# Seven-product units in the first halves alone, and their weight sums as VectorE additions

## The chip, the core and the metric

The kernel runs on one core of a Trainium2 chip, in one launch. A core has TensorE (the matrix multiplier, PE in the profile; PEld is its loading of stationary operands), VectorE (DVE), ScalarE (ACT), GpSimd (POOL) and SyncE (SP), which here only issues transfers. Each engine works through its own instructions in order and waits for others by semaphores. Transfers from the device's main memory are issued from the queues of SP and POOL (a few from ACT) and carried by 16 DMA engines. Matrix products accumulate in PSUM; everything else lies in SBUF. The metric is the device time of an execution in microseconds (us).

## The reference

A bidirectional encoder of two layers on a sequence of 256 tokens of width 2048, in 32-bit floats. Layer 0 mixes tokens by grouped-query attention with rotary positions, layer 1 by dilated windowed attention. Both are followed by the same kind of gated MLP, which is where the change lies:

```
def conv_ffn(h, w_up, conv_w, conv_b, w_down):
    u = h @ w_up                       # [256, 2048] @ [2048, 2 * 5632]
    u = lax.conv_general_dilated(u, conv_w[:, None, :], window_strides=(1,), padding=((1, 1),),
                                 dimension_numbers=('NWC', 'WIO', 'NWC'), feature_group_count=c) + conv_b
    gate, val = jnp.split(u, 2, axis=-1)
    return (jax.nn.silu(gate) * val) @ w_down      # [256, 5632] @ [5632, 2048]

h = h + conv_ffn(rms_norm(h, ffn_norm[i]), w_up[i], conv_w[i], conv_b[i], w_down[i])
```

After the second layer a last RMS norm gives the output.

## The kernel before

**Splitting.** A 32-bit product is made of three products of rounded operands. Each weight tile `raw` (128 partitions x 1024 numbers, 512 KB) is split by ScalarE into a rounded high part `wh` and by VectorE into the rest, `wl = raw - wh`. Each operand of the activations is split once in the same way (`xh`, `xl`). TensorE then adds `xh*wh`, `xh*wl` and `xl*wh`, three matmuls of 128 x 128 by 128 x 512 each. `wh` and `wl` have four buffers each (`NHL`). In the down-projections the raw tiles have six buffers: four, and two more that every third tile takes (`raw_tile`), so a load may be issued once the tile six places ahead of it is used up.

**An ordinary chunk.** `feed` (L102) multiplies a group of 512 rows of a weight matrix ("chunk", `kg`) with one group of 512 columns (`n`). It loads two raw tiles (L114), splits them (L136, L137) and issues 24 matmuls, 12 for each raw tile ("half chunk"; L124 to L126).

**The MLP.** `ffn` (L371) runs the 11 blocks of the inner width in two halves of 6 and 5 (`HALVES`, loop variable `hf`). In each half the blocks are projected up, convolved and gated; the value blocks' results become the stationary operands (`act_split`, L463), and the down-projection of this half follows, four groups of 512 columns that are added to the residual `h`. The work of the activations is written as generators. A matmul stream calls `step` between chunks, which issues the next piece of such work, so that it runs beside the matmuls.

**The seven-product unit.** For a chunk in `fast` (chunks 2 and 3), the pair of column groups `ns` is not done by two times 24 = 48 matmuls. The activations' chunk and the two weight chunks are taken as 2 x 2 blocks, and the eight block products are replaced by seven, of combined operands, in the manner of Strassen and Winograd: 42 matmuls. The activations' combinations are made once (`combined`, L481). The weights' blocks are b11, b12, b21, b22, and four sums of them are needed: t1 = b11 + b12, t3 = b12 + b22, t2 = t1 + b22, t4 = t2 + b21. `fast_unit` (L506) makes the unit in the order b11, b21, b22, t1, t3, t2, t4: a split by ScalarE (L534) and VectorE (L535) and six matmuls (L540 to L542) for each. The seven accumulators are folded into `h` later (`fold`, L546).

t1 and t3 are made by transfers: `load_sum` (L512) loads one block from SP's queue (L509) and then lets a transfer from POOL's queue add the other block on top of it (L514). t2 and t4 are VectorE additions (L531, L533). t1, t2 and t4 lie in the tiles `u` that are free at that time.

**Order.** `pair` (L570) sets the order of chunks for a pair of column groups. In the first half (`hf == 0`) of both layers, for each of two pairs: chunks 0 and 1 ordinary on both sides (eight half chunks), unit of chunk 2, chunk 4 ordinary on both sides (four half chunks), unit of chunk 3, chunk 5 ordinary. That makes eight units. In the second half of layer 1 alone (`last`), the first pair of column groups has two units more, with ordinary chunks between them; `plain_too` (L498) then makes plain halves of these chunks' activations too, for the column groups 2 and 3, which run ordinarily (`project` and, for the last, `project_last`). The second half of layer 0 has no units: `project2` runs column groups 0 and 1, `project` 2 and 3.

The order of instructions on each engine is not that of the text. A scheduler places them when the program is built, by priorities (`tc.high_priority(offset=AHEAD)` lifts the splits and the sums beside them) and by a model of when operands and buffers come free. `tc.keep_in_program_order` ties the places of single instructions.

Of the kernel before, what the change touches and what calls it, by code (L numbers as in the profile page):

```python
# [30 lines left out]
def tile_encoder(ctx: ExitStack, tc: tile.TileContext, x, xT, w_a, w_ao, q_gain, k_gain, w_b, w_bo,  # L31
                 rel_bias, gains, w_up, conv, w_down, final_norm, rope, ident_c, onehot, out):
    nc = tc.nc
# [211 lines left out]
    def pair_slot(kt, shape, dt=F32, name="pr"):  # L245
        return hpool.tile(shape, dt, tag=f"a{kt // 2}", name=nm(name))
# [124 lines left out]
    def ffn(l, hT, ss_in, cw, g_next, last, side=None):  # L371
        with tc.tile_pool(name=nm("fpool"), bufs=1) as fp:
# [90 lines left out]
            def act_split(value):  # L463
                slots, k0 = value[5:]
                cv = value[2]
                if k0 // 4 in fast:
                    slots[-1 - k0 // 4], *rest = combined(cv, k0)
                    if hf == 1:
                        plain_too(k0, 20 + 2 * fast.index(k0 // 4), *rest)
                    ready.add(k0 // 4)  # L470
                    yield
                    return
                for j in range(4):
                    hi, lo = slots[k0 + j]
                    tc.keep_in_program_order(nc.scalar.activation(hi, cv[:, j, :], AF.Copy))
                    nc.vector.tensor_tensor(lo, cv[:, j, :], hi.bitcast(F32), ALU.subtract)
                    if j == 1:
                        yield
                ready.add(k0 // 4)

            def combined(cv, k0):  # L481
# [14 lines left out]
                return pick, v, sx  # L496

            def plain_too(k0, spot, v, sx):  # L498
                c = pair_slot(spot, [P, 2, 2, P], F32R, "c")
                split_in_order(c[:, 0], c[:, 1], v[:, 0, :, 1])  # L500
                for kt in range(4):
                    b, j = divmod(kt, 2)
                    one = (sx[:, 4, j], sx[:, 5, j]) if b else (c[:, 0, j], c[:, 1, j])
                    slots[k0 + kt] = (sx[:, b, j], one[0]), (sx[:, 2 + b, j], one[1])

            def fast_unit(acc, pick, wap0, wap1, begun, end):  # L506
                def load(wap, i, r=None):
                    r = r or raw_tile()
                    nc.sync.dma_start(r.rearrange("p a c -> p (a c)"), wap[:, i * 1024:(i + 1) * 1024])  # L509
                    return r  # L510

                def load_sum(wapx, i, wapy, k, r=None):  # L512
                    r = load(wapx, i, r)
                    nc.gpsimd.dma_start(r.rearrange("p a c -> p (a c)"), wapy[:, k * 1024:(k + 1) * 1024],  # L514
                                        accum_op=ALU.add)
                    return r

                def spot(i):
                    return u_tile(i)[:, :1024].rearrange("p (a c) -> p a c", a=2)

                t1 = load_sum(wap0, 0, wap1, 0, spot(0))
                b11 = load(wap0, 0)
                t3 = load_sum(wap1, 0, wap1, 1)
                b21, b22 = load(wap0, 1), load(wap1, 1)
                t2, t4 = spot(1), spot(2)
                for i, (q, r) in enumerate(((1, b11), (2, b21), (3, b22), (5, t1), (7, t3), (6, t2), (4, t4))):
                    wh = spool.tile([P, 2, 512], F32R, tag="wh", name=nm("wh"), bufs=NHL)
                    wl = spool.tile([P, 2, 512], F32R, tag="wl", name=nm("wl"), bufs=NHL)
                    with tc.high_priority(offset=AHEAD):
                        if q == 6:  # L530
                            nc.vector.tensor_tensor(t2, t1, b22, ALU.add)  # L531
                        if q == 4:
                            nc.vector.tensor_tensor(t4, t2, b21, ALU.add)  # L533
                        nc.scalar.activation(wh, r, AF.Copy)  # L534
                        nc.vector.tensor_tensor(wl, r, wh.bitcast(F32), ALU.subtract)  # L535
                    xh, xl = pick[q]
# [33 lines left out]
            def pair(wd, ns, lhs, order, done, hurry=False):  # L570
# [4 lines left out]
                for i, (kg, side) in enumerate(order):  # L575
# [22 lines left out]
                        if pending:  # L598
                            step()
                    if end:  # L600
                        while beside and hf == 1:
                            step(True)
                        done(sides[side], ns[side])

            def flush(value):
# [12 lines left out]
            for hf, (p0, p1) in enumerate(HALVES):  # L618
                slots = {}
                ready.clear()  # L620
                new_us()
                fast = (2, 3) if hf == 0 or last else ()
                last_value = None
                for p in range(p0, p1):
                    k0 = 4 * (p - p0)
# [107 lines left out]
                if hf == 0:  # L733
                    for ns in (0, 1), (2, 3):
                        pair(wd, ns, slots, both[0] + both[1] + f0 + both[4] + f1 + both[5], done, ns[0] == 0)
                    continue
# [609 lines left out]
```

## Time and profile before

| | us |
|---|---|
| median of three runs | 2271.96 |
| lowest, highest | 2268.68, 2272.84 |
| profiled execution | 2274.03 |
| its span, first to last instruction | 2272.2 |
| TensorE with a matmul in work | 2241.3 (99%) |
| VectorE busy | 1688.0 (74%) |
| ScalarE busy | 1266.0 (56%) |
| GpSimd busy | 756.2 (33%) |

All figures of views come from the one profiled execution. Its mean granted TensorE clock is 0.995. Matmuls overlap: a row gives about 390 ns for one, but they start some 227 ns apart, so rates are to be taken from starts and not from durations. A busy TensorE is therefore one that has no hole, not one at its peak. "Busy" of an engine leaves out what its queue does, such as issuing transfers. A time in brackets behind a row of the timeline is idle time of that engine just before it, and what ended it.

### The profile page before, as it was taken

How to read it: one execution, taken by the hardware profiler on the slowest of the kernel's cores; microseconds unless marked ns; L12 is line 12 of the kernel's file. 1: busy time of each engine (PE TensorE's matmuls, PEld its weight loads, DVE VectorE, ACT ScalarE, POOL GpSimd, SP SyncE). 2: the span in 40 equal slices, each digit the busy share in tenths (PEclk: the TensorE clock that was granted, in tenths of full speed). 3: DMA queues.
4: the chain of work that ended last, by engine and by line, in shares of the span. 5: the costliest groups of instructions: out<-in, count | busy, mean ns of one | idle time of the engine just before them, and what ended most of it. 6: DMA issues, size and time to landing. Idle time of an engine off the chain costs nothing.

```text
span 2272.2 us, 28705 instructions
## 1 busy us (share of the span) xinstructions
PE 2241.3 (99%) x10029; PEld 1852.9 (82%) x10029; DVE 1688.0 (74%) x2251; ACT 1266.0 (56%) x1754; POOL 756.2 (33%) x991
## 2 busy tenths in 40 slices
PE   9999999999999999999999999999999989999998
PEld 7888888887778888888888888888888877888877
DVE  6877867776766776878887887676768777676784
ACT  7576556556545656555454554445656645465653
POOL 3342065671006553010061007003666400356611
PEclk9999999999999999999999999999999999999999
DMA  8665665657766665566656555566655677565674
GB/s 302 193 216 179 216 196 189 194 194 210 241 220 191 194 194 194 186 196 200 185 189 194 186 176 177 184 203 201 200 196 193 204 232 231 192 196 192 215 230 135
DMA packets 130369, 455.30 MB, mean 200 GB/s; under 512 B 14760, under 2 KB 18600, under 8 KB 130224
## 3 DMA queue, kind: packets, MB, share of 16 engines
q1 hardware_dynamic: 124496, 434.30, 58.2%
q0 software_dynamic: 5440, 18.88, 4.2%
q8 instruction: 78, 1.28, 0.2%
q14 instruction: 67, 0.55, 0.1%
q10 hardware_dynamic: 288, 0.30, 0.0%
HBM read 448.07 MB, written 5.34 MB: 200 GB/s over the span
## 4 chain that ended last, share of the span: by engine, by line
PE 89%; DMA 4%; DVE 3%; POOL 2%; issue 1%; ACT 1%; SPq 0%; DVEq 0%; POOLq 0%; ACTq 0%
PE acc L125 28%; PE acc L124 28%; PE acc L126 28%; DMA u<-in_w_down_dram 2%; POOL wide L272 2%; DMA raw<-in_w_down_dram 1%; DVE wl L535 1%; DVE wl L137 1%; DMA raw<-in_w_a_dram 1%; PE ps L541 1%; PE ps L542 0%; PE acc L541 0%; PE ps L540 0%; ACT wh L136 0%; PE acc L542 0%
## 5 line engine op out<-in xcount | busy, mean ns | idle before, releaser
L137 DVE TENSOR_TENSOR wl<-raw,wh 128x1024 fp32r<-128x1024 f32 (+1 forms) x764 | 952.3, 1252 | 396.0 <-ACT wh L136 391.2
L136 ACT ACTIVATE wh<-raw 128x1024 fp32r<-128x1024 f32 (+1 forms) x764 | 799.5, 1050 | 707.0 <-PE acc L126 629.0
L124 PE MATMUL acc<-wh,xh 128*128 128x512 f32 x2176 | 849.6, 391 | 0.0
L125 PE MATMUL acc<-wl,xh 128*128 128x512 f32 x2176 | 848.8, 390 | 0.7 <-DVE wl L137 0.6
L126 PE MATMUL acc<-wh,xh 128*128 128x512 f32 x2176 | 848.6, 390 | 0.0
L432 POOL COPY u<-quad 32x256 f32<-32x256 f32 x672 | 477.3, 710 | 340.2 <-DVE quad L268 313.8
L125 PEld LDWEIGHTS acc<-wl,xh 128*128 128x128 f32 x2176 | 409.2, 188 | 85.4 <-DVE wl L137 2.4
L126 PEld LDWEIGHTS acc<-wh,xh 128*128 128x128 f32 x2176 | 409.0, 188 | 84.9
L124 PEld LDWEIGHTS acc<-wh,xh 128*128 128x128 f32 x2176 | 409.5, 188 | 83.7 <-ACT wh L136 0.3
L124 PE MATMUL acc<-wh,a 128*128 128x512 f32 x824 | 321.5, 390 | 0.5 <-ACT wh L136 0.5
L125 PE MATMUL acc<-wl,a 128*128 128x512 f32 x824 | 321.0, 390 | 0.0
L126 PE MATMUL acc<-wh,a 128*128 128x512 f32 x824 | 321.0, 390 | 0.0
L124 PEld LDWEIGHTS acc<-wh,a 128*128 128x128 f32 x824 | 154.7, 188 | 32.4 <-ACT wh L136 0.8
L126 PEld LDWEIGHTS acc<-wh,a 128*128 128x128 f32 x824 | 154.7, 188 | 32.2 <-DVE a L219 0.2
L125 PEld LDWEIGHTS acc<-wl,a 128*128 128x128 f32 x824 | 154.8, 188 | 31.8 <-DVE wl L137 0.2
L272 POOL COPY wide<-quad 32x256 f32<-32x256 f32 x165 | 107.2, 650 | 171.8 <-DVE quad L268 162.7
L368 ACT ACTIVATE stg<-acc,rstd 128x512 f32<-128x512 f32 x122 | 82.8, 684 | 32.8 <-PE acc L126 32.8
L449 POOL TENSOR_TENSOR cv<-cg,cv 128x1024 f32<-128x1024 f32 x18 | 57.9, 3216 | 108.3 <-DVE cv L419 108.3
L419 DVE SCALAR_TENSOR_TENSOR cg<-u,cw,cg 128x256 f32<-128x256 f32 x176 | 82.2, 511 | 4.5 <-ACT cg L411 4.5
L402 POOL MEMSET u<- 128x4 f32 x12 | 1.0, 106 | 228.9 <-ACT junk L258 188.3
L419 DVE SCALAR_TENSOR_TENSOR cv<-u,cw,cv 128x256 f32<-128x256 f32 x176 | 73.7, 478 | 2.8 <-ACT cv L411 2.7
L534 ACT ACTIVATE wh<-raw 128x1024 fp32r<-128x1024 f32 x40 | 42.2, 1058 | 51.7 <-PE acc L126 23.5
(246 smaller groups left out, 1684.4 us busy)
## 6 DMA issues: line engine op xcount, KB each, us to landing
raw<-in_w_up_dram SPq DMA_DIRECT2D x352, 512.0 KB, 4.6
raw<-in_w_down_dram SPq DMA_DIRECT2D x176, 512.0 KB, 4.8
raw<-in_w_b_dram SPq DMA_DIRECT2D x144, 512.0 KB, 4.3
raw<-in_w_bo_dram SPq DMA_DIRECT2D x48, 512.0 KB, 3.8
raw<-in_w_a_dram SPq DMA_DIRECT2D x40, 512.0 KB, 4.7
raw<-in_w_ao_dram SPq DMA_DIRECT2D x32, 512.0 KB, 4.4
raw<-in_w_down_dram POOLq DMA_DIRECT2D x10, 512.0 KB, 8.8
u<-in_w_down_dram SPq DMA_DIRECT2D x10, 512.0 KB, 5.9
```

The source lines that it names most:

```text
L124: nc.tensor.matmul(accs[m], xh, wh[:, j, :], start=st, stop=False)
L125: nc.tensor.matmul(accs[m], xh, wl[:, j, :], start=False, stop=False)
L126: nc.tensor.matmul(accs[m], xl, wh[:, j, :], start=False, stop=sp)
L136: nc.scalar.activation(wh[:, c], r[:, c], AF.Copy)
L137: nc.vector.tensor_tensor(wl[:, c], r[:, c], wh[:, c].bitcast(F32), ALU.subtract)
L272: nc.gpsimd.tensor_copy(o[32 * c:32 * c + 32, :, 32 * q:32 * q + 32], quad[32 * q:32 * q + 32, c])
L368: nc.scalar.activation(o[:, m, :], accs[m], AF.Copy, scale=rstd[:, m:m + 1])
L419: nc.vector.scalar_tensor_tensor(cj, halves(flat[:, j, o:o + NT])[:, ::-1], tap(n, j, i), cj, ALU.mult, ALU.add)
L432: nc.gpsimd.tensor_copy(o, src)
L449: made.append(eng.tensor_tensor(cv, cg, cv, ALU.mult).ins)
L534: nc.scalar.activation(wh, r, AF.Copy)
L535: nc.vector.tensor_tensor(wl, r, wh.bitcast(F32), ALU.subtract)
```

## The change

Three things are changed.
- Layer 1's second half has no units any more. `fast` is empty there, and its down-projection takes the way of layer 0's second half: `project2` for column groups 0 and 1, `project` for 2; `project_last` stays for 3. `plain_too` goes.
- In the eight units left, no transfer adds. A unit loads its four blocks once each from SP's queue, in the order b11, b21, b22, b12.
- All four sums are VectorE additions, written directly in front of the split that reads them: t1 into a `u` tile, b12 + b22 in place of b12, t2 and t4 into `u` tiles. The order of the seven products is the same.

```
     if k0 // 4 in fast:
-        slots[-1 - k0 // 4], *rest = combined(cv, k0)
-        if hf == 1:
-            plain_too(k0, 20 + 2 * fast.index(k0 // 4), *rest)
+        slots[-1 - k0 // 4] = combined(cv, k0)
...
 def fast_unit(acc, pick, wap0, wap1, begun, end):
...
-    def load_sum(wapx, i, wapy, k, r=None):
-        r = load(wapx, i, r)
-        nc.gpsimd.dma_start(r.rearrange("p a c -> p (a c)"), wapy[:, k * 1024:(k + 1) * 1024],
-                            accum_op=ALU.add)
-        return r
...
-    t1 = load_sum(wap0, 0, wap1, 0, spot(0))
-    b11 = load(wap0, 0)
-    t3 = load_sum(wap1, 0, wap1, 1)
-    b21, b22 = load(wap0, 1), load(wap1, 1)
-    t2, t4 = spot(1), spot(2)
-    for i, (q, r) in enumerate(((1, b11), (2, b21), (3, b22), (5, t1), (7, t3), (6, t2), (4, t4))):
+    b11, b21, b22, b12 = load(wap0, 0), load(wap0, 1), load(wap1, 1), load(wap1, 0)
+    t1, t2, t4 = (spot(i) for i in range(3))
+    sums = {5: (t1, b11, b12), 7: (b12, b12, b22), 6: (t2, t1, b22), 4: (t4, t2, b21)}
+    for i, (q, r) in enumerate(((1, b11), (2, b21), (3, b22), (5, t1), (7, b12), (6, t2), (4, t4))):
...
         with tc.high_priority(offset=AHEAD):
-            if q == 6:
-                nc.vector.tensor_tensor(t2, t1, b22, ALU.add)
-            if q == 4:
-                nc.vector.tensor_tensor(t4, t2, b21, ALU.add)
+            if q in sums:
+                nc.vector.tensor_tensor(*sums[q], ALU.add)
             nc.scalar.activation(wh, r, AF.Copy)
             nc.vector.tensor_tensor(wl, r, wh.bitcast(F32), ALU.subtract)
...
-    fast = (2, 3) if hf == 0 or last else ()
+    fast = (2, 3) if hf == 0 else ()
...
     if not fast:
         done(project2(wd, 0, 1, slots, rest, 1, lambda a: done(a, 0)), 1)
         for n in (2, 3):
-            done(project(wd, n, slots, rest), n)
+            if last and n == 3:
+                project_last(wd, n, slots, rest, first_out, last_out)
+            else:
+                done(project(wd, n, slots, rest), n)
         continue
...
-    pair(wd, (0, 1), slots, both[0] + [(1, 0)] + f0 + [(1, 1)] + f1 + both[4], done, True)
-    done(project(wd, 2, slots, list(range(np_))), 2)
-    project_last(wd, 3, slots, list(range(np_)), first_out, last_out)
```

More of the change, by code (lines that the diff above doesn't have):

```diff
@@ L495, in combined, with load @@
                     pick[q] = own[0][:, i], own[1][:, i]
[L496 to L504, printed above, removed]
+                return pick
             def fast_unit(acc, pick, wap0, wap1, begun, end):
-                def load(wap, i, r=None):
-                    r = r or raw_tile()
+                def load(wap, i):
+                    r = raw_tile()
                     nc.sync.dma_start(r.rearrange("p a c -> p (a c)"), wap[:, i * 1024:(i + 1) * 1024])
-                    return r
-                def load_sum(wapx, i, wapy, k, r=None):
-                    r = load(wapx, i, r)
-                    nc.gpsimd.dma_start(r.rearrange("p a c -> p (a c)"), wapy[:, k * 1024:(k + 1) * 1024],
-                                        accum_op=ALU.add)
                     return r
@@ L600, in pair @@
                     if end:
-                        while beside and hf == 1:
-                            step(True)
                         done(sides[side], ns[side])
```

6 lines of the change are left out of this document (2 added, 4 removed).

## The prediction

> **What bounds the kernel now.** I read the page first, then the busy sums of the ten stretches in which the seven-product units run, then the timeline of one of them, the waits, and the landings of the loads.
>
> The page, span and engines:
>
> ```profile
> span 2272.2 us, 28705 instructions
> ...
> PE 2241.3 (99%) x10029; PEld 1852.9 (82%) x10029; DVE 1688.0 (74%) x2251; ACT 1266.0 (56%) x1754; POOL 756.2 (33%) x991
> ```
>
> TensorE is the bound: only 31 us of the span are without a matmul. So the change is worth what it does to the number of matmuls and to the holes between them. The holes sit in the units. Busy sums by stretch; each of the first ten runs from a unit's first matmul to the one behind its last, the eleventh is ordinary work:
>
> ```profile
> core 0: us, PE busy (x) PEld busy (x) DVE busy (x) ACT busy (x) POOL busy (x), PEclk, DMA share, GB/s
> 542.69:557.48 14.79, 11.62 (x43) 8.87 (x42) 9.18 (x9) 7.00 (x7) 0.89 (x1) 0.88 0.60 165
> 568.39:580.12 11.73, 10.18 (x44) 7.74 (x42) 11.73 (x12) 7.93 (x8) 0.00 (x0) 1.00 0.79 258
> 612.83:622.50 9.67, 9.67 (x44) 7.90 (x42) 9.10 (x9) 7.45 (x7) 0.86 (x1) 1.00 0.91 286
> 633.41:647.00 13.59, 10.19 (x44) 7.74 (x42) 12.82 (x12) 8.84 (x9) 0.32 (x3) 1.00 0.52 186
> 1816.91:1833.32 16.41, 12.54 (x43) 9.40 (x42) 9.54 (x10) 7.08 (x7) 1.72 (x2) 0.79 0.61 167
> 1844.23:1857.86 13.63, 11.62 (x43) 8.66 (x42) 13.17 (x12) 8.86 (x9) 0.35 (x1) 0.87 0.68 225
> 1890.53:1900.20 9.67, 9.67 (x44) 7.90 (x43) 7.46 (x7) 7.43 (x7) 1.72 (x2) 1.00 0.80 252
> 1911.10:1922.55 11.45, 10.20 (x44) 7.74 (x42) 11.45 (x11) 7.92 (x8) 0.32 (x3) 1.00 0.59 191
> 2167.38:2180.63 13.25, 11.28 (x46) 8.04 (x44) 12.35 (x15) 7.97 (x11) 0.92 (x2) 1.00 0.64 211
> 2185.64:2198.63 12.99, 10.83 (x43) 7.51 (x42) 10.14 (x10) 7.38 (x8) 0.00 (x0) 1.00 0.82 260
> 800.00:1000.00 200.00, 200.00 (x884) 165.66 (x883) 151.63 (x214) 115.44 (x162) 57.45 (x76) 1.00 0.59 191
> ```
>
> Two units run without a hole: 42 matmuls in 9.67 us. The eight of the first halves (layer 0, then layer 1) take 100.94 us together, 23.6 more than eight times 9.67. Ordinary matmuls follow each other every 200 / 883 = 0.2265 us, also in the second half of layer 0, which the last row crosses and which has no units. What makes the holes is seen in the first unit (timelines of SP, POOL, VectorE, TensorE):
>
> ```profile
> 536.91 0.33 SPq L509 DMA_DIRECT2D u<-in_w_down_dram  x1
> 542.74 0.89 POOL L514 DMA_DIRECT2D u<-in_w_down_dram  x1 [12.43 <-DVE wl L535]
> 548.26 1.23 DVE L531 TENSOR_TENSOR u<-u,raw 128x1024 f32<-128x1024 f32 x1 [5.54 <-DMA u<-in_w_down_dram]
> 549.46 0.51 PE L540 MATMUL ps<-wh,s 128*128 128x512 f32 x1 [2.42 <-ACT wh L534]
> 550.72 0.79 PE L541 MATMUL ps<-wl,s 128*128 128x512 f32 x1 [0.76 <-DVE wl L535]
> ```
>
> The sum t1 is a load from SP and behind it an adding transfer from POOL. Issued at 542.74, it lands 5.5 us later; VectorE, in order, stands before t2 (L531) for it, ScalarE before the split, TensorE behind both. By the waits this is the rule in the units:
>
> ```profile
> DVE u L531 <- DMA u<-in_w_down_dram: 31.4, 6, 8.3
> DVE u L531 <- DMA raw<-in_w_down_dram: 25.4, 4, 8.2
> ```
>
> All ten L531 waited for a transfer, 5.7 us each on average.
>
> **The change part by part.**
>
> *Second half of layer 1 without units.* Two units, 84 matmuls, become 96 ordinary ones: 96 x 0.2265 = 21.7 us. Their stretches last 13.25 + 12.99 = 26.24, less two ordinary matmuls inside the first (44 weight loads, not 42), 0.45: 25.8. Gain 4.1 us, in which 12 more matmuls (2.7) are already paid. The outer work that goes (combining the activations, a copy of their plain halves, folding the accumulators) and what replaces it (eight plain splits) lie beside some 10.9 us of matmuls per chunk (48 x 0.2265) and count nothing; if that cover were short it would be a row or two of VectorE, about 1 us. The order that takes their place is that of layer 0's second half, which had no hole in the row above; bound 0 to 2 us.
>
> *Transfers.* In the eight units left, each issues four loads from SP where it had five and none from POOL where it had two adding ones. Nothing on POOL's queue or on SP's waits behind them any more. A b11 tile now comes free after t1 instead of after its split, and so the second next chunk's load starts later; that load is needed a whole unit later and hides.
>
> *VectorE.* Per unit 7 splits + 4 sums instead of 7 + 2. Rows: three splits in a row, then the first unit as it ran (VectorE, and one ScalarE):
>
> ```profile
> 611.21 3.49 DVE L535 TENSOR_TENSOR wl<-raw,wh 128x1024 fp32r<-128x1024 f32 x3
> 536.75 1.22 DVE L535 TENSOR_TENSOR wl<-raw,wh 128x1024 fp32r<-128x1024 f32 x1
> 537.89 1.22 DVE L449 TENSOR_TENSOR cv<-cg,cv 128x1024 f32<-128x1024 f32 x1
> 539.03 1.22 DVE L535 TENSOR_TENSOR wl<-raw,wh 128x1024 fp32r<-128x1024 f32 x1
> 540.16 1.43 DVE L476 TENSOR_TENSOR a<-cv,a 128x256 fp32r<-128x256 f32 x4
> 541.50 1.22 DVE L535 TENSOR_TENSOR wl<-raw,wh 128x1024 fp32r<-128x1024 f32 x1
> 540.39 1.05 ACT L534 ACTIVATE wh<-raw 128x1024 fp32r<-128x1024 f32 x1
> ```
>
> One whole-tile operation every 1.14 us: 11 x 1.14 = 12.5 us for a unit of 9.67. VectorE loses 2.9 us per unit and must bring it as a lead. It has one: four split buffers let it stand three splits ahead, and a sum needs no split buffer, so it fills the time VectorE waits for one (an ordinary half chunk is 12 x 0.2265 = 2.72 us of TensorE for 1.14 of VectorE). In the built order the sums do not stand directly in front of their splits in every unit:
> - First unit of each layer: split 1, the product cv (L449), t1, split 2, an a split, t3, split 3, three a splits, split of t1, t2, split of t3, t4, split 6, split 7. From the row at 536.75 split 6 ends after 11 large ones and four a's: 536.75 + 11 x 1.14 + 1.43 = 550.7; TensorE, which began the unit at 542.69, takes 9.67 / 7 = 1.38 us per product and wants the low half of the sixth one matmul behind its start: 542.69 + 5 x 1.38 + 0.23 = 549.8. Hole about 1.0 us where there were 5.12 and 6.74; split 7, at 551.9, is in time again.
> - Second unit of the first pair: t1 comes behind split 1, then six more operations up to the split of t1, which is wanted 4.4 us into the unit. 7 x 1.14 + 0.08 = 8.1, so the last load must have landed 3.7 us before the unit begins. It takes the buffer of the second half chunk behind the first unit, split two operations after split 7 (551.9 + 2 x 1.14 = 554.2), and the unit begins at 542.69 + 9.67 + 1.0 + 10.87 = 564.2: 6.3 us for the landing.
> - Second pair, first unit: t1 is pulled in front of the last ordinary split, and seven operations lead from it to split 2, wanted 1.6 us into the unit: t1 must start 8.1 - 1.6 = 6.5 us ahead. The fourth load of the second row below goes out at 590.86 + 8.48 - 0.33 = 599.0, the unit begins at 612.83: the landing has 7.3 us.
> - Second pair, second unit: t1 stands in front of split 1, all four sums in front of split 3, which is wanted 3.0 us into the unit: seven operations, 5.1 us ahead. Here VectorE is not behind, so the buffer comes free with TensorE's product 5 (6.9 us into the first unit), one ScalarE and one VectorE operation later: 9.2. The unit begins at 9.67 + 10.87 = 20.5 on that clock: 20.5 - 5.1 - 9.2 = 6.2 us.
>
> So the price hangs on the loads:
>
> ```profile
> 521.15 9.68 SPq L509 DMA_DIRECT2D raw<-in_w_down_dram  x4
> ...
> 590.86 8.48 SPq L509 DMA_DIRECT2D raw<-in_w_down_dram  x4
> ...
> raw<-in_w_down_dram SPq DMA_DIRECT2D x176, 512.0 KB, 4.8
> ...
> raw<-in_w_down_dram POOLq DMA_DIRECT2D x10, 512.0 KB, 8.8
> ...
> DMA to landing us min/median/max: 3.4/5.7/11.0
> ```
>
> A plain load of these weights lands in 4.8 us (median), those of the units (last line, L509) in 5.7, at most 11.0, where the adding ones (8.8) ran beside them. These go, and three of seven transfers of a unit, so I take 5: in time everywhere. The ends are no hole at all and, at 11.0, the third rival. For near misses I take 0.2 us in each of six units. Holes left: 2 x 1.0 + 6 x 0.2 = 3.2 of 23.6: gain 20.4 us.
>
> The Trainium skill, "VectorE: DVE Perf Modes", section "The DRAIN you can't avoid", says the next operation does not start until the pipe has emptied. By it the eleven operations would stand 1.22 apart instead of 1.14, about 0.9 us more in each first unit and 1.8 us off the gain. The row of three splits (3.49 us, not 3.66) decides against it.
>
> *Sum.* -20.4 - 4.1 = -24.5 us. The profiled execution took 2274.03 us, 1.8 beside its span: 2249.5. It was 2.07 above the median of the three runs, 2271.96, so in the median 2247.5 us.
>
> **The rivals.**
> 1. Loads land in about 8 us, because those of the second units are still issued close behind each other. Then the second units stall 1.8 us each, the second pair's first ones 0.7, with 2.0 as before: 10.6 left, gain 13.0 + 4.1: 2254.9. For it: the 11.0 above; against: 4.8 for the same load elsewhere.
> 2. The lead is not there and VectorE paces every unit: 8 x (12.54 - 9.67) = 23.0, and in each first unit the product and four a's, 1.14 + 1.43, twice: 5.1. Holes 28.1 against 23.6, less 4.1: 2272.4, no change. For it: VectorE is busy for all of 11.73 us in the second row; against: there it had just stood still for a transfer, and in the two rows with 9.67 it was busy for 9.10 and 7.46 only.
> 3. Slower: VectorE stands in front of a sum that was pulled ahead, while the last load is late, and everything behind it stands too. At 11.0 us the second units lose 4.8 each and the second pair's first ones 3.7. Long holes cost more than themselves: in the first unit waits of 2.42 + 0.76 made 5.12, with the granted clock at 0.88, so 1.9 us more each. 4 x 6.7 + 2 x 5.6 + 2.0 = 40.0 against 23.6, less 4.1: 2284.3. It decides from a landing of about 9 us, where 27.7 us of holes eat both gains.
> 4. The transfers were not what held the units, and the holes stay at half, 12 us: 2256. Against: the L531 waits.
>
> **How the numbers follow.** Forecast 2247.5 with 0.70, its own range 2243 to 2253. Rivals 1 and 4 together 0.17, rival 2 0.06, rival 3 0.07. A measurement tells about 0.2% (4.5 us) from no change: faster 0.87, same 0.06, slower 0.07. Range 2241 to 2259: it leaves out rivals 2 and 3 and some of rival 4.
>
> **What would show it.** Right: no adding transfer on POOL; the four sums at 1.14 to 1.22 us; TensorE's waits for split operations down to a few us, the largest in each layer's first unit, around 1 us, before split 6; stretches of units near 9.7 us; no hole in layer 1's second half; 12 more matmuls. Wrong: VectorE waiting several us before a sum for a transfer (rivals 1, 3), or units of 12 us with VectorE busy throughout (rival 2).

## The result, and the profile after

The changed kernel takes 2247.91 us (median of four runs, 2246.75 to 2249.16) against 2270.32 (2267.42 to 2272.84) for the kernel before on the same chip: a ratio of 0.9902, 95% interval 0.9885 to 0.9919. Measured again beside later experiments it took 2247.64 us against 2274.14, a ratio of 0.9883 (0.9866 to 0.9899). The forecast was 2247.5. The kernel before varies more from one execution to the next (2267.42 to 2281.0 us over all runs) than the changed one (2246.0 to 2249.16), so the gain in medians is 22.4 us in the first measurement and 26.5 in the second.

In the changed kernel the loads of a unit are line L499, the sums L513, the splits L514 (ScalarE) and L515 (VectorE), the matmuls L520 to L522. The page, span and engines:

```profile
span 2246.0 us, 28619 instructions
...
PE 2233.1 (99%) x10041; PEld 1852.2 (82%) x10041; DVE 1686.5 (75%) x2241; ACT 1259.0 (56%) x1747; POOL 733.0 (33%) x971
```

The span is 26.2 us shorter than the 2272.2 of before, with 12 more matmuls. Busy sums by stretch, one row per unit (layer 0's four, the first and the last of layer 1), and the last row adds up all eight:

```profile
core 0: us, PE busy (x) PEld busy (x) DVE busy (x) ACT busy (x) POOL busy (x), PEclk, DMA share, GB/s
542.60:553.29 10.69, 10.09 (x43) 7.73 (x42) 10.62 (x13) 6.92 (x7) 0.00 (x0) 1.00 0.46 142
564.19:573.85 9.66, 9.66 (x43) 7.89 (x42) 9.45 (x9) 7.81 (x8) 0.00 (x0) 1.00 0.52 179
606.52:616.18 9.66, 9.66 (x43) 7.89 (x42) 7.45 (x7) 7.44 (x7) 0.00 (x0) 1.00 0.51 174
627.09:636.76 9.67, 9.67 (x44) 7.89 (x42) 9.26 (x9) 7.81 (x8) 0.31 (x3) 1.00 0.52 174
1806.67:1817.37 10.70, 10.08 (x44) 7.73 (x43) 10.63 (x13) 6.94 (x7) 0.00 (x0) 1.00 0.45 154
...
1891.16:1900.83 9.67, 9.67 (x44) 7.89 (x42) 9.29 (x9) 7.81 (x8) 0.31 (x3) 1.00 0.53 177
sum 79.38, PE 78.17 PEld 62.80 DVE 73.65 ACT 59.98 POOL 0.63; mean PE 9.77 PEld 7.85 DVE 9.21 ACT 7.50 POOL 0.08
```

Six units run in 9.66 or 9.67 us, without a hole; the first unit of each layer takes 1.0 us more. The holes are 79.38 - 8 x 9.67 = 2.0 us, where the same eight units had 23.6. The granted clock is 1.00 in every row, where three of the same eight rows of before had 0.88, 0.79 and 0.87. This gives 21.6 of the 26.2 us. From the last matmul of the last unit of layer 1's first half to the end of the span it was 2272.2 - 1922.55 = 349.65 us before and is 2246.0 - 1900.83 = 345.17 now: 4.5 us, from the second half without units. Together 26.1.

How VectorE makes the first unit (timeline, VectorE):

```profile
545.96 1.22 DVE L513 TENSOR_TENSOR u<-u,raw 128x1024 f32<-128x1024 f32 x1
547.09 1.22 DVE L515 TENSOR_TENSOR wl<-raw,wh 128x1024 fp32r<-128x1024 f32 x1
548.23 1.21 DVE L513 TENSOR_TENSOR u<-u,raw 128x1024 f32<-128x1024 f32 x1
549.36 2.51 DVE L515 TENSOR_TENSOR wl<-u,wh 128x1024 fp32r<-128x1024 f32 x2
```

Sums and splits start 1.13 to 1.14 us apart without a pause. The splits of products 6 and 7 come last, and TensorE waits for the sixth (timeline, TensorE):

```profile
549.65 0.39 PE L520 MATMUL ps<-wh,s 128*128 128x512 f32 x1
550.63 0.50 PE L521 MATMUL ps<-wl,s 128*128 128x512 f32 x1 [0.60 <-DVE wl L515]
```

The 0.60 in brackets counts from the end of the row above, and rows overlap. From start to start the gap is 0.98 us where 0.23 is usual; the rest of the 1.0 us lies in smaller gaps of the same stretch.

The transfers behind it: what VectorE waited for in front of sums (the waits: in total, times, longest), and the landings of the units' loads:

```profile
DVE u L513 <- DMA raw<-in_w_down_dram: 9.6, 6, 2.1
```

```profile
DMA to landing us min/median/max: 3.4/4.4/5.2
```

VectorE does stand before a sum for a load, in six places, 1.6 us on average. These are the six units without a hole: the splits made before had given TensorE enough to do.

### The profile page after: what moved, and what is told of

Same layout as the page of the kernel before. It is cut to its first block, busy times and chain, and to the rows that moved or that the text cites. A ratio compares the mean times of both kernels' runs of the same rounds, so it can differ in the third digit from the quotient of the medians.

```text
span 2246.0 us, 28619 instructions
## 1 busy us (share of the span) xinstructions
PE 2233.1 (99%) x10041; PEld 1852.2 (82%) x10041; DVE 1686.5 (75%) x2241; ACT 1259.0 (56%) x1747; POOL 733.0 (33%) x971
## 4 chain that ended last, share of the span: by engine, by line
PE 93%; DVE 3%; POOL 2%; issue 1%; ACT 1%; DMA 1%; SPq 0%; DVEq 0%; POOLq 0%; ACTq 0%
PE acc L125 29%; PE acc L126 29%; PE acc L124 29%; POOL wide L272 2%; PE ps L521 1%; DMA raw<-in_w_a_dram 1%; PE ps L522 1%; DVE wl L515 1%; PE ps L520 1%; DVE wl L137 1%; PE acc L521 0%; PE acc L522 0%; PE acc L520 0%; PE ps L234 0%; PE ps L233 0%
## 5 line engine op out<-in xcount | busy, mean ns | idle before, releaser
L136 ACT ACTIVATE wh<-raw 128x1024 fp32r<-128x1024 f32 (+1 forms) x772 | 807.8, 1050 | 721.4 <-PE acc L126 645.8
L124 PE MATMUL acc<-wh,a 128*128 128x512 f32 x880 | 343.0, 390 | 0.0
L125 PE MATMUL acc<-wl,a 128*128 128x512 f32 x880 | 342.5, 389 | 0.0
L126 PE MATMUL acc<-wh,a 128*128 128x512 f32 x880 | 342.5, 389 | 0.0
L126 PEld LDWEIGHTS acc<-wh,a 128*128 128x128 f32 x880 | 165.1, 188 | 34.5 <-DVE a L219 0.2
L125 PEld LDWEIGHTS acc<-wl,a 128*128 128x128 f32 x880 | 165.2, 188 | 33.9
L124 PEld LDWEIGHTS acc<-wh,a 128*128 128x128 f32 x880 | 165.3, 188 | 33.8
L419 DVE SCALAR_TENSOR_TENSOR cg<-u,cw,cg 128x256 f32<-128x256 f32 x176 | 82.2, 510 | 4.5 <-ACT cg L411 4.5
L419 DVE SCALAR_TENSOR_TENSOR cv<-u,cw,cv 128x256 f32<-128x256 f32 x176 | 73.6, 477 | 2.8 <-ACT cv L411 2.8
L268 DVE STREAM_TRANSPOSE quad<-stg 128x512 f32<-128x512 f32 x88 | 59.0, 696 | 8.6 <-ACT stg L368 8.6
```

What stands on the lines that cost most here:

```text
L124: nc.tensor.matmul(accs[m], xh, wh[:, j, :], start=st, stop=False)
L125: nc.tensor.matmul(accs[m], xh, wl[:, j, :], start=False, stop=False)
L126: nc.tensor.matmul(accs[m], xl, wh[:, j, :], start=False, stop=sp)
L136: nc.scalar.activation(wh[:, c], r[:, c], AF.Copy)
L268: nc.vector.transpose(quad[:, :, at, :], src.rearrange("p (x c t) -> p c x t", c=4, t=32))
L419: nc.vector.scalar_tensor_tensor(cj, halves(flat[:, j, o:o + NT])[:, ::-1], tap(n, j, i), cj, ALU.mult, ALU.add)
```

## The experiments

Nine kernels, and the changed one once more. "Units" is the length of the stretches of the eight units of the first halves together (the first figure of the row that begins with "sum"), "holes" what it has over 8 x 9.67 = 77.4 us. In some kernels an ordinary matmul or two stand within a stretch, so holes are good to 1 or 2 us. Each ratio is to the kernel before as it was measured beside that run (medians from 2270.32 to 2275.51 us), not to the first row; runs that were not taken beside each other are better compared by their ratios and their profiles than by their medians.

| kernel | units, us | holes, us | median, us | ratio to before (95%) |
|---|---|---|---|---|
| before (profiled run) | 100.94 | 23.6 | 2270.32 | 1 |
| changed | 79.38 | 2.0 | 2247.91 | 0.9902 (0.9885 to 0.9919) |
| changed, again | | | 2247.64 | 0.9883 (0.9866 to 0.9899) |
| sums only | 79.37 | 2.0 | 2250.93 | 0.9890 (0.9873 to 0.9907) |
| second half only | 95.24 | 17.9 | 2268.49 | 0.9980 (0.9966 to 0.9994) |
| sums pinned | 131.41 | 54.1 | 2298.92 | 1.0107 (1.0088 to 1.0125) |
| two more sums | 91.53 | 14.2 | 2257.62 | 0.9924 (0.9907 to 0.9942) |
| same traffic | 85.88 | 8.5 | 2253.53 | 0.9910 (0.9896 to 0.9925) |
| one adding transfer | 93.40 | 16.0 | 2260.55 | 0.9939 (0.9925 to 0.9954) |
| four raw buffers | 84.53 | 7.2 | 2254.77 | 0.9910 (0.9895 to 0.9926) |
| later first unit | 77.75 | 0.4 | 2247.45 | 0.9882 (0.9868 to 0.9897) |
| units in layer 0's second half | | | 2267.67 | 0.9968 (0.9954 to 0.9982) |

### The two parts alone

The sums on VectorE alone: the kernel before with the new `fast_unit`, units still in layer 1's second half.

```
-    t1 = load_sum(wap0, 0, wap1, 0, spot(0))
...
+    b11, b21, b22, b12 = load(wap0, 0), load(wap0, 1), load(wap1, 1), load(wap1, 0)
+    t1, t2, t4 = (spot(i) for i in range(3))
+    sums = {5: (t1, b11, b12), 7: (b12, b12, b22), 6: (t2, t1, b22), 4: (t4, t2, b21)}
...
     fast = (2, 3) if hf == 0 or last else ()
```

> One part alone: the four weight sums on VectorE, four loads from SP, no adding transfer, in all ten units; the second half of layer 1 keeps its two units. Theory (the adding transfers made the holes): the eight units of the first halves as in the changed kernel, 2.0 us of holes against 23.6. In the second half VectorE has the last block's work in the first unit besides (eight convolution steps, product, splits), so holes of about 3.7 us there and 1.3 us in the second unit: 19.3 + 5.0 = 24.3 us for the two where ordinary chunks take 21.7. Time about 2250 us, 2 to 3 us above the changed kernel, 20 to 22 below the kernel before. Rival (most of the gain came from the second half's units going): about 2260 us or more.

Measured 2250.93 us. The median is 3.0 us above that of the changed kernel, but the ratios to the kernel before (0.9890 here, 0.9902 and 0.9883 there) cannot tell the two apart; the profile can. Its stretches: the last unit of layer 1's first half, the sum of all eight of the first halves, and the two units of layer 1's second half:

```profile
core 0 of [0], span 2249.8 us
...
1890.47:1900.14 9.67, 9.67 (x44) 7.89 (x43) 9.20 (x9) 7.81 (x8) 0.31 (x3) 1.00 0.50 177
sum 79.37, PE 78.14 PEld 62.80 DVE 73.72 ACT 59.95 POOL 0.63; mean PE 9.77 PEld 7.85 DVE 9.22 ACT 7.49 POOL 0.08
...
2144.96:2159.67 14.71, 12.35 (x44) 9.05 (x43) 14.71 (x18) 8.47 (x11) 0.00 (x0) 0.88 0.39 124
2164.92:2175.89 10.97, 10.36 (x44) 7.84 (x43) 10.94 (x11) 7.47 (x8) 0.00 (x0) 1.00 0.55 185
```

The first halves are those of the changed kernel. In the second half the units keep their holes, some 6 us (14.71 + 10.97 - 2 x 9.67 = 6.3, less an ordinary matmul or two), although no transfer adds there either: VectorE is busy for the whole of the first one (14.71 of 14.71 us, 18 operations), with the last block's product and pieces among splits and sums. From the end of the last first-half unit (1900.14) to the end of the span it is 349.66 us, as in the kernel before (349.65) and 4.5 us more than in the changed kernel (345.17). So VectorE sums do nothing for these two units, and what is gained there comes from giving them up.

The second half alone: the changed kernel with the old `fast_unit` and its adding transfers in the first halves.

```
     fast = (2, 3) if hf == 0 else ()
...
+    t1 = load_sum(wap0, 0, wap1, 0, spot(0))
+    b11 = load(wap0, 0)
+    t3 = load_sum(wap1, 0, wap1, 1)
```

> The other part alone: no units in the second half of layer 1, the eight units of the first halves with their adding transfers as before. Theory: holes of 23.6 us stay, 4.1 us are gained: ratio 0.998, about 2266 us. Rival: 2255 us or less, if the second half was what mattered.

Measured 2268.49 us over 12 runs (2264.03 to 2277.11). The last of the eight units and their sum:

```profile
core 0 of [0], span 2262.3 us
...
1904.76:1917.10 12.34, 10.19 (x43) 7.73 (x42) 12.34 (x12) 7.92 (x8) 0.32 (x3) 1.00 0.58 196
sum 95.24, PE 84.52 PEld 65.39 DVE 79.39 ACT 60.73 POOL 6.80; mean PE 10.57 PEld 8.17 DVE 9.92 ACT 7.59 POOL 0.85
```

The holes of the adding transfers are there, 17.9 us. The profiled execution is the fastest of the twelve (2264.03 us, 4.5 below the median), so an ordinary one has more. That they are 5.7 fewer than in the profile of before, with the same code, and that this kernel's runs spread over 13 us where the changed kernel's eight spread over 3.2, suggests that the old units' holes differ from one execution to the next; it was not followed further. The tail behind the last unit (1917.10) is 345.2 us, as in the changed kernel: the two parts are separate, about 22 us and 4.5.

### What the sums' place on VectorE is worth

The sums and the splits on VectorE were tied to the order of the text, each sum directly in front of its split, so that the scheduler could pull none ahead.

```
-    nc.vector.tensor_tensor(*sums[q], ALU.add)
+    tc.keep_in_program_order(nc.vector.tensor_tensor(*sums[q], ALU.add))
     nc.scalar.activation(wh, r, AF.Copy)
-    nc.vector.tensor_tensor(wl, r, wh.bitcast(F32), ALU.subtract)
+    tc.keep_in_program_order(nc.vector.tensor_tensor(wl, r, wh.bitcast(F32), ALU.subtract))
```

> The changed kernel, but each sum is held directly in front of its split in VectorE's order, as the text has it, where the scheduler had pulled it ahead. Theory: then every sum, the ScalarE operation on it and the split behind that stand in a row, 1.2 + 1.1 + 1.2 us with their waits about 3.6 us per product, for 1.38 us of TensorE. From t1 on that gives holes of about 0.9, 2.2 and 2.1 us in each of the eight units, 5.2 us together, 42 us in all against 2.0: about 2288 us, more if the clock falls. Rival (only the count of VectorE's operations matters, 11 for a unit in any order): at most 0.8 us per unit, about 2252 us.

Measured 2298.92 us: slower than the kernel before by 1.1%, and 11 us beyond what was expected. The stretches of the eight units, and the timelines of VectorE and of ScalarE in one of them:

```profile
sum 131.41, PE 102.99 PEld 68.94 DVE 94.80 ACT 58.07 POOL 0.63; mean PE 12.87 PEld 8.62 DVE 11.85 ACT 7.26 POOL 0.08
```

```profile
622.78 1.23 DVE L515 TENSOR_TENSOR wl<-raw,wh 128x1024 fp32r<-128x1024 f32 x1 [1.26 <-ACT wh L514]
623.92 1.22 DVE L513 TENSOR_TENSOR u<-u,raw 128x1024 f32<-128x1024 f32 x1
626.34 1.23 DVE L515 TENSOR_TENSOR wl<-u,wh 128x1024 fp32r<-128x1024 f32 x1 [1.20 <-ACT wh L514]
```

```profile
625.25 1.06 ACT L514 ACTIVATE wh<-u 128x1024 fp32r<-128x1024 f32 x1 [2.51 <-DVE u L513]
```

A pinned sum makes a round trip: sum on VectorE, split on ScalarE, which must wait for it, split on VectorE, which waits for ScalarE. VectorE can do nothing in between, for the next sum stands behind. One product takes 626.34 - 622.78 = 3.56 us this way, where TensorE wants one every 1.38. The same four sums cost 6.5 us per unit more than where the scheduler places them. The two units that kept a granted clock of 1.00 have holes of 6.0 and 6.2 us, where 5.2 were expected; in the other six the clock was 0.77 to 0.97 and the holes are 6.1 to 8.3 us.

### How much room VectorE has

The additions of t2 and t4 were done twice, with the same result.

```
     if q in sums:
         nc.vector.tensor_tensor(*sums[q], ALU.add)
+        if q in (6, 4):
+            nc.vector.tensor_tensor(*sums[q], ALU.add)
```

> The changed kernel with the additions t2 and t4 made twice, 13 whole-tile operations of VectorE per unit in place of 11, 2.3 us more. Theory (the lead hides them where nothing else is on VectorE): the first unit of each layer gets all of it, holes of 3.3 us in place of 1.0; the second units about 0.5 us each, the second pair's first ones none: about 6.8 us more, 2254.7 us. Rival (VectorE paces every unit): 8 x 2.3 = 18 us more, 2266 us.

Measured 2257.62 us, some 10 us more than the changed kernel, where about 7 were expected. Layer 1's first unit and the sum of the eight stretches, then a VectorE row of layer 0's first unit (there the second additions are L515, the splits L516 and L517):

```profile
1811.20:1825.37 14.17, 11.21 (x45) 7.83 (x43) 12.93 (x15) 6.83 (x7) 0.00 (x0) 1.00 0.36 121
...
sum 91.53, PE 83.82 PEld 63.97 DVE 85.62 ACT 57.82 POOL 0.63; mean PE 10.48 PEld 8.00 DVE 10.70 ACT 7.23 POOL 0.08
```

```profile
553.31 1.23 DVE L517 TENSOR_TENSOR wl<-u,wh 128x1024 fp32r<-128x1024 f32 x1 [1.20 <-ACT wh L516]
```

Two operations of 1.14 us more have no cover in a first unit. They cost more than themselves because here the last sum ends up directly in front of its split, and VectorE waits 1.20 us for the round trip over ScalarE. The first units took 4.6 and 3.5 us more than in the changed kernel (2.3 were expected), the second units of the first pairs 1.2 and 2.1 (0.5 were expected), and three of the other four nothing: VectorE does not pace every unit.

### Traffic or the adding transfer

First the traffic: three plain loads more in each unit, seven times 512 KB as before the change.

```
+    more = [spot(i) for i in range(3)]
+    for r, (wap, i) in zip(more, ((wap0, 0), (wap1, 0), (wap1, 1))):
+        nc.sync.dma_start(r.rearrange("p a c -> p (a c)"), wap[:, i * 1024:(i + 1) * 1024])
     b11, b21, b22, b12 = load(wap0, 0), load(wap0, 1), load(wap1, 1), load(wap1, 0)
-    t1, t2, t4 = (spot(i) for i in range(3))
+    t1, t2, t4 = more
```

> The changed kernel, but each unit issues three plain loads more from SP's queue, into the three tiles that the sums t1, t2, t4 are written to afterwards (what they bring is overwritten by the sums and is used by nothing). So each unit moves seven times 512 KB, as before the change, with no transfer that adds. My theory (the holes of before came from waiting for a load and then for an adding transfer behind it, not from the amount of traffic): the sums t1 and t4 come somewhat later because of the loads under them, holes of 0 to 8 us in all, 2248 to 2256 us. Rival (seven transfers in a unit are too much for the queues, whatever kind they are): most of the 20 us comes back, 2262 us or more, with VectorE and ScalarE waiting for landings of 8 us and more in the units.

Measured 2253.53 us, 5.9 more than the changed kernel beside it. The stretches, the landings of the units' ordinary four loads (L499), and what ScalarE's splits in the units waited for most:

```profile
sum 85.88, PE 80.90 PEld 62.79 DVE 78.25 ACT 58.79 POOL 0.63; mean PE 10.11 PEld 7.85 DVE 9.78 ACT 7.35 POOL 0.08
```

```profile
DMA to landing us min/median/max: 3.4/4.7/8.7
```

```profile
ACT wh L517 <- DVE u L516: 12.2, 7, 3.2
```

The longest landing is 8.7 us, against 5.2 in the changed kernel, and the holes grow by 6.5 us. About half of the growth is in the first unit of each layer. There TensorE waited for ScalarE's splits alone, and ScalarE for the sums alone; VectorE had stood 1.4 us in front of the first sum for the load under it. Over all units ScalarE waited 17.6 us for sums (8.0 in the changed kernel) and 7.0 for loads (none there). So late sums come first and late loads second. The traffic as such accounts for at most a part of the old 23.6.

Then one adding transfer: t1 made by a load and a transfer that adds, as before the change, the other three sums on VectorE.

```
-    b11, b21, b22, b12 = load(wap0, 0), load(wap0, 1), load(wap1, 1), load(wap1, 0)
     t1, t2, t4 = (spot(i) for i in range(3))
-    sums = {5: (t1, b11, b12), 7: (b12, b12, b22), 6: (t2, t1, b22), 4: (t4, t2, b21)}
+    nc.sync.dma_start(t1.rearrange("p a c -> p (a c)"), wap0[:, :1024])
+    nc.gpsimd.dma_start(t1.rearrange("p a c -> p (a c)"), wap1[:, :1024], accum_op=ALU.add)
+    b11, b21, b22, b12 = load(wap0, 0), load(wap0, 1), load(wap1, 1), load(wap1, 0)
+    sums = {7: (b12, b12, b22), 6: (t2, t1, b22), 4: (t4, t2, b21)}
```

> The changed kernel, but t1 is again a load from SP with an adding transfer from POOL behind it; the other three sums stay on VectorE, so VectorE has one operation fewer per unit. Theory (the adding transfer is late, and VectorE, which holds t2 in front of other splits, stands before it): 6 to 18 us of holes come back, 2254 to 2265 us, and VectorE's waits for the u tile's transfer are in front of t2. Rival (one adding transfer is early enough, it was the two together or the number of transfers): holes under 3 us, 2246 to 2250 us.

Measured 2260.55 us, 12.9 more. The stretches and the landings of the eight adding transfers, then the first unit: what SP waited for before it issued t1's load (L506), that load, the adding transfer (L507), VectorE and TensorE (sums L515, high-part matmuls L522):

```profile
sum 93.40, PE 84.67 PEld 66.11 DVE 76.03 ACT 60.03 POOL 5.65; mean PE 10.58 PEld 8.26 DVE 9.50 ACT 7.50 POOL 0.71
```

```profile
DMA to landing us min/median/max: 5.4/8.4/9.3
```

```profile
SPq L506 <- DVE cv L419: 2.0, 1, 2.0
```

```profile
536.43 0.33 SPq L506 DMA_DIRECT2D u<-in_w_down_dram  x1
541.98 0.93 POOL L507 DMA_DIRECT2D u<-in_w_down_dram  x1 [15.86 <-DMA u<-in_w_down_dram]
547.45 1.23 DVE L515 TENSOR_TENSOR u<-u,raw 128x1024 f32<-128x1024 f32 x1 [5.21 <-DMA u<-in_w_down_dram]
```

```profile
548.64 0.80 PE L522 MATMUL ps<-wh,s 128*128 128x512 f32 x1 [3.10 <-ACT wh L516]
```

VectorE is less busy than with the three plain loads (76.03 of 93.40 us, 81%, against 78.25 of 85.88, 91%), and still stands 5.21 us for the adding transfer, in front of t2, as in the kernel before. One such transfer per unit, with five loads in place of four, brings back more than half of the holes; it costs 12.9 us against 5.9 for three plain loads, which move more bytes. So it is mainly the adding transfer behind a load that holds a unit.

The rows also say when it does. The tile of t1 comes free late, with the last block's convolution (`cv`, L419). From there the load and the adding transfer take 547.45 - 536.43 = 11.0 us, one after the other, and the unit begins at 541.19. A sum on VectorE needs the tile for one operation of 1.22 us. Of the 16.0 us of holes 12.5 are in the first unit of each layer (16.83 and 15.01 us long). Where t1's tile is free early, the same transfer costs nothing: in layer 0's third unit it goes out at 579.92 and the unit begins at 611.61, and the first units of the second pairs take 9.66 and 9.67 us here, and 9.67 in the kernel before.

### Later loads

Four raw buffers instead of six: `extra[0] = None` in place of `extra[0] = fp`.

> The changed kernel with four buffers for the raw weight tiles in the down-projections instead of six, so each load goes out only when the tile four places ahead of it is used up, which is about one half chunk or product and a half to three later than before; the work is the same. Theory (what keeps the units whole is that the last load of a unit lands before VectorE comes to the sum that was pulled ahead; my third rival's mechanism): holes in both units of a pair, 1.0, 1.2, up to 4 and 1.1 us in the four units of a layer, 4 to 13 us more in all than the changed kernel, 2252 to 2261 us, with VectorE waiting for the raw tiles' transfers in front of sums. Rival (the loads have so much slack that two buffers fewer cost nothing): 2247 to 2250 us.

Measured 2254.77 us, not beside the changed kernel. The ratios to the kernel before are 0.9910 and 0.9883, some 6 us apart, and the profiled span is 5.5 us longer. The stretches (the first unit of layer 0's second pair, the longest of all, and the sum), and VectorE's waits in front of sums:

```profile
607.76:617.67 9.91, 9.91 (x43) 7.81 (x42) 9.91 (x9) 7.45 (x7) 0.00 (x0) 1.00 0.53 182
...
1809.06:1820.73 11.67, 10.46 (x43) 7.66 (x42) 11.60 (x14) 6.14 (x6) 0.00 (x0) 1.00 0.46 152
...
sum 84.53, PE 80.75 PEld 62.07 DVE 83.96 ACT 55.71 POOL 0.63; mean PE 10.09 PEld 7.76 DVE 10.50 ACT 6.96 POOL 0.08
```

```profile
DVE u L513 <- DMA raw<-in_w_down_dram: 12.6, 7, 3.0
```

Every unit now has a hole, 0.2 to 2.0 us, most under 1.1, and 5.2 us more in all. In seven of the eight TensorE waits for a split of VectorE (3.7 us in all). The mechanism of the third rival is there, with a small price: the first units of the second pairs, for which up to 4 us were expected, lost 0.2 and 0.5.

### A later first unit

For the first pair of column groups: one column group of chunk 4 ahead of the first unit.

```
-    pair(wd, ns, slots, both[0] + both[1] + f0 + both[4] + f1 + both[5], done, ns[0] == 0)
+    if ns[0] == 0:
+        seq = both[0] + both[1] + [(4, 0)] + f0 + [(4, 1)] + f1 + both[5]
+    else:
+        seq = both[0] + both[1] + f0 + both[4] + f1 + both[5]
+    pair(wd, ns, slots, seq, done, ns[0] == 0)
```

> The changed kernel, but in the first pair of column groups of each layer one ordinary column group of chunk 4 (24 matmuls, 5.4 us) is done ahead of the first unit and only the other one between the two units; the second pair is as it was. Theory (the hole of about 1.0 us in each layer's first unit comes from the last block's product and its splits, which stand on VectorE among the unit's splits): that hole goes, because this work now lies beside ordinary matmuls; between the units VectorE has 5.4 us for two splits of 1.14 us, wins back 3.1 us and so makes good the 2.9 that a unit costs it. No hole in any unit, about 2 us less than the changed kernel: 2246 us, a ratio of 0.999 to it, which the profile can show and the clock hardly. Rival (the lead of the second unit came from the 10.9 us of ordinary work between the units): holes of 1 to 3 us in the second unit of the first pair of each layer, 2248 to 2253 us.

Layer 0's first two units, and the sum over all eight:

```profile
547.99:557.65 9.66, 9.66 (x43) 7.89 (x42) 8.15 (x8) 7.44 (x7) 0.00 (x0) 1.00 0.54 178
563.12:573.12 10.00, 9.99 (x44) 7.81 (x43) 9.97 (x9) 7.80 (x8) 0.00 (x0) 1.00 0.59 201
...
sum 77.75, PE 77.74 PEld 62.96 DVE 69.94 ACT 60.99 POOL 0.63; mean PE 9.72 PEld 7.87 DVE 8.74 ACT 7.62 POOL 0.08
```

The hole of the first units is gone, so it was the last block's work among the unit's operations; VectorE had 8 operations in that stretch instead of 13. The second unit, with 24 ordinary matmuls ahead of it instead of 48, loses 0.3 us, in layer 1 0.1. In the profile 1.6 us of holes go; the median, 2247.45 us (2246.09 to 2248.93), cannot be told from the changed kernel's 2247.64 of the same hour. It is the kernel with the fewest holes of all that were tried.

### More units

On top of that, units in layer 0's second half, where there were none. The fold is finished before the residual's squares are taken.

```
-    fast = (2, 3) if hf == 0 else ()
+    fast = (2, 3) if hf == 0 or not last else ()
...
+    while hf == 1 and beside:
+        step(True)
     add_residual(accs, n)
...
+    if hf == 1:
+        seq = both[0] + [(1, 0)] + f0 + [(1, 1)] + f1 + both[4]
```

> The kernel with the later first unit, and besides it units of the new kind in the second half of layer 0 too, which had none: both pairs of column groups there, chunks in the order 0, first column group of 1, unit of 2, second column group of 1, unit of 3, 4. Four units more, 4 times 6 matmuls fewer, 24 times 0.2265 us = 5.4 us. Theory (a unit with VectorE sums costs 9.67 us where VectorE has 5.4 us of ordinary work ahead of it): holes of 0 to 2 us in all, 2242 to 2244 us, a ratio of 0.986 to the kernel before. Rival (in this half fewer ordinary chunks lie ahead of the first unit, the last block's product and the combinations of the activations come while it runs, and the norm and the transposes of the next stage have to wait for the folding): holes of 1 to 3 us in each unit take all of the gain, 2247 us or more.

Measured 2267.67 us, 20 more than without these units. The stretch of the third new unit, VectorE in it (L277 is a transpose for the next stage) and behind the four units, and a wait of TensorE there:

```profile
939.03:957.00 17.97, 13.35 (x46) 9.14 (x44) 17.48 (x22) 7.34 (x8) 0.00 (x0) 0.91 0.35 117
```

```profile
943.12 1.22 DVE L513 TENSOR_TENSOR u<-raw,raw 128x1024 f32<-128x1024 f32 x1
944.37 0.43 DVE L277 STREAM_TRANSPOSE tT<-h 32x256 f32<-32x256 f32 x1
...
989.62 5.39 DVE L277 STREAM_TRANSPOSE tT<-h 32x256 f32<-32x256 f32 x12
```

```profile
PE acc L125 <- DVE wl L137: 4.0, 1, 4.0
```

The rival's side, and more than it said. These units share VectorE with the transposes of the residual that follow each finished column group; VectorE is busy for 17.48 of 17.97 us, and behind the units TensorE waits another 4.0 us while twelve transposes in a row stand ahead of a split. The four new units are 12.5, 11.1, 18.0 and 13.2 us long. The 5.4 us of saved matmuls are lost several times over.

## Why the prediction was right

**The clean unit and what held the old ones.** The clean unit of 9.67 us came six times out of eight. That the holes came mainly from the adding transfers is shown from both sides: without them 2.0 us are left, one per unit puts 14 back, and plain loads of the old amount 6.5, in part by late sums. The runs do not separate the new order of a unit's loads from the rest, nor how slow an adding transfer would be without the loads beside it.

**The second half of layer 1.** Predicted gain 4.1 us, measured 4.5 in the tail of the span, the same in the kernel that made this part alone (tail 345.2, ratio 0.998). The activations' work that fell away was counted as nothing. Not foreseen was that VectorE sums would not have helped these two units.

**VectorE's lead.** The forecast rested on the scheduler's order, with sums pulled ahead. The first unit's hole was worked out as 1.0 us before the sixth split and was 1.0 in both layers; that split was said to end at 550.7 and ended at 549.36 + 1.22 = 550.6. The Trainium skill ("VectorE: DVE Perf Modes", section "The DRAIN you can't avoid") lets the next operation start only when the pipe is empty, which the prediction read as 1.22 us apart; the same section adds that an operation that is not held starts earlier. The rows above are 1.13 to 1.14 apart, which agrees with the addition; the measurement decided, as the prediction had taken it.

**Landings.** Taken as 5 us with 6.2 to 7.3 allowed, they were 4.4 at the median and 5.2 at most, so all six other units were in time. The near misses, 0.2 us in each of six units, did not occur: these 1.2 us are the term that was wrong, together with the 0.4 us of the second half and 0.1 in the rest. The span is 26.2 us shorter where 24.5 was predicted.

**From the profile to the median.** 2249.5 was predicted for a profiled execution and 2247.76 measured. The step to the median took off 2.07 us, since the profiled run of before stood so far above its median; the changed kernel's profiled run is 0.15 us under its own. The miss of the sum and this step have opposite signs, and 2247.5 came nearer to the measured 2247.91 than its parts did. That it came within 0.4 us is luck; that it came within some 2 us is not.

**Rivals.** Landings of 8 us (rival 1) came back only in the kernel with three loads more (8.7 us at most) and where a transfer adds again (8.5 with one per unit). Rival 4 (the transfers were not the cause) fell. Rival 3, VectorE standing before a pulled-ahead sum, happens (9.6 us in six places) but hidden; with loads issued later the holes grew by 5 us. Its price of 40 was for landings of 11.0 us; there they were 5.7 at most, so that price was not put to the test. (Its 1.9 us for the lower clock was some 1.5: in the first unit of before the two waits are 2.6 and 1.0 us longer than usual from start to start, not 2.42 and 0.76.) Rival 2 was the most dangerous and its price was wrong: it counted only VectorE's busy time, 12.5 us per unit, and so gave 2272.4. A sum that really stands directly in front of its split costs the round trip over ScalarE, 3.56 us per product, and the kernel with all of them pinned took 2298.9. Of the kernels that ran, only this one ended slower than before. That it did not come about in the changed kernel is due to the scheduler's order, which the prediction had read.

**Two figures for transfers.** The Trainium skill ("DMA: Bandwidth & Descriptors", section "Anatomy of one DMA — SWDGE (gpsimd) path") gives 2.0 us plus the bytes at 436 per nanosecond for a transfer from GpSimd, 3.2 us for these 512 KB; it says nothing there of what adding costs. The adding transfers landed in 5.4 to 9.3 us (median 8.4) in the kernel with one per unit, beside other loads; an estimate by that figure makes them look harmless. It fits six plain transfers of this size that GpSimd issued in the kernel before (`there<-quad`, median 3.4 us), but not one other (`oc`, 6.6 us), and not those that add.

## What to carry to other kernels

A sum that feeds a split on two engines is not priced by the time of its engine alone: look where the scheduler puts it, because directly in front of its consumer it costs the round trip (3.56 us here), and far enough ahead it costs its own 1.14. A transfer that adds on top of another comes after both landings (11.0 us here), which matters where its tile comes free shortly before it is wanted; there an addition on an engine with a lead was cheaper, even though it made that engine busier. And a saving in matmuls was worth taking here only where the engine that prepares the operands had ordinary work ahead of it: the units ran nearly without holes in the first halves, two of them lost 4.5 us in layer 1's second half, and four lost 20 us in layer 0's.

## What the runs showed of the hardware that was not expected

The granted clock falls after several short holes as well as after a long one (behind the wait of 4.0 us in the kernel with more units it was 0.50 from 996 to 1000 us). In the kernel with pinned sums a stretch of 7 us within a unit, and the waits of TensorE's matmuls from there to 633 us:

```profile
623.00:630.00 7.00, 4.92 (x13) 2.71 (x12) 4.59 (x5) 2.24 (x3) 0.00 (x0) 0.74 0.48 158
```

```profile
624.06 0.50 PE L521 MATMUL ps<-wl,s 128*128 128x512 f32 x1 [0.76 <-DVE wl L515]
626.36 0.79 PE L520 MATMUL ps<-wh,s 128*128 128x512 f32 x1 [0.86 <-ACT wh L514]
627.62 0.79 PE L521 MATMUL ps<-wl,s 128*128 128x512 f32 x1 [0.47 <-DVE wl L515]
```

No wait is longer than 0.86 us (1.26 us from the start of one matmul to the next), and the clock is 0.74 of full over the stretch. The Trainium skill ("TensorE: Matmul & The Clock Gate", section "What's actually happening") has the half rate follow at least one idle window of about 3.4 us; here no idle time of that length is seen, TensorE is only busy for 4.92 of 7.00 us. The first unit of the same kernel has waits of up to 0.90 us, with TensorE busy for 11.61 of 15.67 us, and kept 1.00. So did a unit of 14.17 us, TensorE busy for 11.21, in the kernel with two more sums (the row is shown there). Holes of the same size were followed by a lower clock in one unit and not in another, so these runs give no bound from which it falls.
